# A two-layer encoder on 8 cores: transposes moved to the host, weight slabs stored contiguously, one projection reordered

## The chip, the cores and the metric

One Trainium2 chip, all 8 cores, each with its own 2048 tokens. The metric is device time in microseconds of the slowest core. In some executions the cores of one die, or of both, are granted a lower TensorE clock and the run is some per cent longer.

## The reference, cut to what matters

```python
D_MODEL, BATCH, SEQ, N_MEM, D_FF = 1024, 2, 8192, 256, 2816
# layer 0: conv mixer; layer 1: chunked spatial gating. Each layer:
x = x + mixer(rms_norm(x, g_mix))                       # in-proj, mixing, output projection
x = x + memory_cross_attention(rms_norm(x, g_xattn), rms_norm(mem, g_mem), w_q, w_k, w_v, w_o)
x = x + swiglu(rms_norm(x, g_ffn), w_gate, w_up, w_down)
# after both layers
out = rms_norm(x, g_final)                              # (2, 8192, 1024) float32
```

A core does its 2048 tokens in two halves of 1024, each half in two tiles of 512, with features on the partitions. x of a half stays in SBUF as `hT` (fp32), its norm as `nT` (bf16), and all weights are streamed once per half.

## The kernel before: the parts that matter

x comes in token by token, so every 128x128 block is transposed on TensorE and copied out of PSUM; the output goes the same way back.

```python
# load_x, tile(tb), one of 8 blocks of 128 tokens, each half hf of the features
ins = e.transpose(ps[:, i * 128:(i + 1) * 128], x.t[:, dc * 128:(dc + 1) * 128], self.ident[:, :])
...                                   # x.t: one of three staging buffers
P.add("act" or "dve", ...)            # copy PSUM -> hT   (shortened)
# store_pieces, piece(tt, tb): the same from nf, through PSUM and four staging buffers, to out
```

A weight slab is a block of columns cut out of a row-major matrix, cast to bf16 on its way, into one of a ring of four buffers. A load waits until the slab four places earlier has been used for the last time.

```python
NS = 4
def ld(self, w2d, c0, cw, kc, after=()):
    i = self.ws_i % NS
    ...
    src = w2d[:, c0:c0 + cw].rearrange("(k p) c -> p k c", p=128)
    self.P.add("pool", lambda e: e.dma_start(out=view, in_=src), ..., dma=f"w{i}")
```

The output projection of a mixer adds to `hT` and starts the next norm at once: squares on ScalarE and their sums on TensorE as each output block is done; after a tile's eighth block, "finish": Ln and Exp on ScalarE, eight scalings on VectorE.

```python
# proj_residual, inside block(slab, ss, s_, cw, tt), for each output block m of tile tt
self.residual_add(b, m, tt)                          # VectorE: hT += PSUM
self.push(j.key, lambda j=j, m=m: j.sq(m), lag)
if m == KC - 1 and not final:
    self.push_finish(j, lag)
...
block(sl0[0], sl0[1], 0, 512, 0)      # tile 0 with both slabs, then tile 1 with both
block(sl1[0], sl1[1], 1, 512, 0)
block(sl0[0], sl0[1], 0, 512, 1)
block(sl1[0], sl1[1], 1, 512, 1)
```

After this projection come the keys (8 groups), the values (4 groups) and the queries (16 groups) of the cross-attention. Keys and values need only the memory; the queries need the new norm. In the ring order the slabs are: two of the output projection, two of keys, two of values, two of queries.

The softmax here doesn't subtract the row's maximum and nothing guards it: scores larger than these inputs give would overflow.

Of the kernel before, what the change touches and what calls it, by code (L numbers as in the profile page):

```python
# [20 lines left out]
XROWS = TH + 2 * HALO  # L21
# [12 lines left out]

class Slot:
# [6 lines left out]

class Op:
    __slots__ = ("eng", "fn", "deps", "idx", "need_inc", "dma", "dma_val")

# [9 lines left out]

class Prog:
    ENGS = ("pe", "act", "dve", "pool", "sp")

    def __init__(self):
        self.streams = {e: [] for e in self.ENGS}  # L60
        self.dma_cnt = {}
        self.final_dma = set()

# [31 lines left out]
    EPOCH = 500  # L95

# [11 lines left out]
    def emit(self, nc, block, esem, dsem):  # L108
        def make(name):
            ops = self.streams[name]  # L110

            def body(e):
                waited = {}
                for o in ops:
# [8 lines left out]
                    for key, (val, h) in need.items():  # L123
                        if key[0] == "e":
                            later = [k for k in waited if k[0] == "e" and k[1] == key[1] and k[2] > key[2]]
                            if later:
                                continue
                        if waited.get(key, 0) < val:
                            e.wait_ge(h, val)
                            waited[key] = val  # L130
# [15 lines left out]

class Buf:
    __slots__ = ("t", "slot", "dma")

    def __init__(self, t, slot, dma=None):  # L150
        self.t = t
        self.slot = slot
        self.dma = dma

class Builder:
    def __init__(self):
# [10 lines left out]
        self.xb = {}  # L167
# [3 lines left out]
    def sb(self, name, shape, dtype):  # L171
        sz = 4 if dtype == F32 else 2
        n = 1
# [4 lines left out]
        self.off = off + n * sz  # L178
# [3 lines left out]
    def _declare_dram(self):  # L182
# [4 lines left out]
        self.x_in = din("x_in", [NHALF, XROWS, D])  # L187
        self.mem = din("mem", [NMEM, D])
        self.vecs = din("vecs", [128, NV])
        self.lnc = din("lnc", [3, D])  # L190
        self.od_w_s = din("od_w_s", [8, 128, 128])
        self.ev_w_in = din("ev_w_in", [D, 2560])
        self.ev_w_out = din("ev_w_out", [D, D])
        self.od_w_in = din("od_w_in", [D, 2048])
        self.od_w_out = din("od_w_out", [D, D])
        self.xa_w = {n: din("xa_w_" + n, [2, D, D]) for n in "qkvo"}
        self.ffn_w_gate = din("ffn_w_gate", [2, D, DFF])
        self.ffn_w_up = din("ffn_w_up", [2, D, DFF])
        self.ffn_w_down = din("ffn_w_down", [2, DFF, D])
        self.out = nc.dram_tensor("out", [TCORE, D], F32, kind="ExternalOutput").ap()  # L200

    def _alloc(self):
# [6 lines left out]
        self.hTh = self.sb("hTh", [128, KC, 2 * HALO], F32)  # L209
        self.hTh_s = [S(f"hTh{k}") for k in range(KC)]  # L210
        self.nTh = self.sb("nTh", [128, KC, 2 * HALO], BF16)
# [8 lines left out]
        self.diagA_s = S("diagA")  # L220
# [6 lines left out]
        self.xs = Ring([Buf(self.sb(f"xs{i}", [128, D], F32), S(f"xs{i}"), f"xs{i}") for i in range(3)])  # L227
# [4 lines left out]
        self.memnT_s = S("memnT")  # L232
        self.junk_s = S("junk")
# [11 lines left out]
        self.mst = self.sb("mst", [128, 2, D], F32)  # L245
        self.mst_s = [S(f"mst{i}") for i in range(2)]
        self.wst = self.sb("wst", [128, 2, 512], F32)
        self.wst_s = [S(f"wst{i}") for i in range(2)]
        self.junk = self.sb("junk", [128, D], BF16)
# [10 lines left out]
        self.xh = self.sb("xh", [2 * HALO, D], F32)  # L260
        self.xh_s = S("xh")
# [25 lines left out]
        self.os = Ring([Buf(self.sb(f"os{i}", [128, D], F32), S(f"os{i}"), f"os{i}") for i in range(4)])  # L287
        u_end = max(u_end, self.off)
        self.off = u_end
        self.union_slot = S("union")  # L290
# [39 lines left out]
    def norm_job(self, key, src_k, src_s, n, gcol, dst_k, dst_s):  # L330
# [3 lines left out]
        def sq(k):  # L334
            if st["b"] is None:
# [3 lines left out]
            ps = self.ps[b]  # L339
# [3 lines left out]
            P.add("act", lambda e: e.activation(out=q.t[:, 0:n], in_=src_k(k), func=AF.Square),  # L343
                  reads=[src_s[k]], writes=[q.slot])
            P.add("pe", lambda e: e.matmul(ps[:, 0:n], lhsT=self.ones[:, :], rhs=q.t[:, 0:n], start=first, stop=last),  # L345
                  reads=[q.slot, self.ones_s], writes=[self.ps_s[b]])
# [6 lines left out]
        def scale(k):  # L353
            r = st["r"]
            P.add("dve", lambda e: e.scalar_tensor_tensor(out=dst_k(k), in0=src_k(k),  # L355
                                                          scalar=self.vec[:, gcol + k:gcol + k + 1],
                                                          in1=r.t[:, 0:n], op0=ALU.mult, op1=ALU.mult),
                  reads=[src_s[k], r.slot, self.vec_s], writes=[dst_s[k]])
# [12 lines left out]
    def main_job(self, tt, gcol, final=False):  # L371
        sl = slice(tt * TT, (tt + 1) * TT)
        if final:
            return self.norm_job(("n", tt), lambda k: self.hT[:, k, sl], [self.hT_s[k][tt] for k in range(KC)], TT,
                                 gcol, lambda k: self.nf[tt][:, k, :], self.nf_s[tt])
        return self.norm_job(("n", tt), lambda k: self.hT[:, k, sl], [self.hT_s[k][tt] for k in range(KC)], TT,
                             gcol, lambda k: self.nT[:, k, sl], [self.nT_s[k][tt] for k in range(KC)])

    def union_switch(self, new_slots):
        pass  # L380
# [14 lines left out]
    def ld(self, w2d, c0, cw, kc, after=()):  # L395
# [3 lines left out]
        view = self.wbuf[i][:, 0:kc * cw].rearrange("p (k c) -> p k c", c=cw)  # L399
        src = w2d[:, c0:c0 + cw].rearrange("(k p) c -> p k c", p=128)  # L400
        self.P.add("pool", lambda e: e.dma_start(out=view, in_=src), reads=list(after), writes=[self.wbuf_s[i]],  # L401
                   dma=f"w{i}")
        return view, self.wbuf_s[i]

    def rstd_bc(self, b, n, scale, eps, extra_sub=None):
        ps = self.ps[b]
        t = self.t32.next()
        if extra_sub is not None:
            self.P.add("dve", lambda e: e.tensor_scalar(out=t.t[:, 0:n], in0=ps[:, 0:n], scalar1=scale, scalar2=eps,
                                                        op0=ALU.mult, op1=ALU.add),  # L410
                       reads=[self.ps_s[b]], writes=[t.slot])
            self.P.add("dve", lambda e: e.tensor_tensor(out=t.t[:, 0:n], in0=t.t[:, 0:n], in1=extra_sub.t[:, 0:n],
                                                        op=ALU.subtract),
                       reads=[t.slot, extra_sub.slot], writes=[t.slot])
            self.P.add("act", lambda e: e.activation(out=t.t[:, 0:n], in_=t.t[:, 0:n], func=AF.Ln),
                       reads=[t.slot], writes=[t.slot])
        else:
            ec = 0 if eps == RMS_EPS else 1
            self.P.add("act", lambda e: e.activation(out=t.t[:, 0:n], in_=ps[:, 0:n], func=AF.Ln, scale=scale,  # L419
                                                     bias=self.epsc[:, ec:ec + 1]),  # L420
                       reads=[self.ps_s[b], self.epsc_s], writes=[t.slot])
        r = self.rsr.next()
        self.P.add("act", lambda e: e.activation(out=r.t[:, 0:n], in_=t.t[:, 0:n], func=AF.Exp, scale=-0.5),  # L423
# [642 lines left out]
    def build(self):  # L1066
# [44 lines left out]
        for f in st:  # L1111
            f()
# [79 lines left out]
```

## Time and profile before

| | before |
|---|---|
| median of 4 runs (range) | 2027.06 us (2024.69 to 2047.15) |
| profiled run, slowest core (core 4) | 2022.6 us |
| TensorE busy on it | 93% |
| packets moved by DMA | 211481 |

The prediction shows the main lines. Three more of the timeline of core 4: two from the second tile's half of the layer-0 output projection, and one of the key matmuls behind it. Columns: start, length, engine, line, operation, operands, count, and in brackets the idle time just before and who ended it.

```profile
229.05 5.34 PE L389 MATMUL ps<-y,wbuf 128*128 128x512 bf16 x24 [2.21 <-ACT t L419]
237.18 0.38 PE L345 MATMUL ps<-sq,ones 128*128 128x512 bf16 x1 [0.42 <-ACT sq L343]
243.73 5.40 PE L389 MATMUL ps<-memnT,wbuf 128*128 128x256 bf16 x48
```

TensorE waits 2.21 us for a PSUM bank that ScalarE still has to read (the Ln of tile 0's norm). The queries start 22 us behind this projection.

### The profile page before, as it was taken

The numbers are of one execution on the slowest core, as the hardware profiler recorded it, in microseconds if no ns is written. First come the engines' busy times: TensorE is split into PE (matmuls) and PEld (weight loads), VectorE is DVE, ScalarE is ACT, GpSimd is POOL, SyncE is SP. The second block draws the span as 40 slices with busy tenths as digits, with TensorE's granted clock in tenths as the row PEclk, the third lists the DMA queues.
The fourth block names the chain that finished last, engine by engine and source line by source line (L and its number), as shares of the span: only waits on it lengthen the run. The fifth ranks groups of instructions, "written<-read, shape, count | busy, mean of one in ns | idle before, by whom it ended". The sixth has DMA issues, their size and how long they took to land.

```text
span 2022.6 us, 25188 instructions; the slowest of 8 cores (2007.9 to 2022.6 us)
## 1 busy us (share of the span) xinstructions
PE 1881.0 (93%) x8942; PEld 882.8 (44%) x9114; DVE 634.8 (31%) x988; ACT 598.9 (30%) x1001; POOL 178.2 (9%) x187
## 2 busy tenths in 40 slices
PE   5699999999989899999979999999998999999997
PEld 3344444444434444444444444444443444344444
DVE  2523415211156334211152432341212651531213
ACT  3323343111133352111152423521111433421112
POOL 6200000001100100001000001000010001000110
PEclk7899999999999999999989998999999999999998
DMA  8052582447736833549546048245497449245482
GB/s 203 7 78 37 76 118 42 65 66 73 81 61 84 114 54 55 71 63 87 68 140 84 1 63 125 42 58 71 60 89 90 61 64 134 32 63 84 50 86 83
DMA packets 211481, 150.91 MB, mean 75 GB/s; under 512 B 93024, under 2 KB 206816, under 8 KB 211360
## 3 DMA queue, kind: packets, MB, share of 16 engines
q0 software_dynamic: 205024, 130.03, 49.9%
q1 hardware_dynamic: 6336, 19.26, 2.8%
q8 instruction: 76, 1.25, 0.3%
q14 instruction: 45, 0.37, 0.1%
HBM read 270.92 MB, written 8.39 MB: 138 GB/s over the span
## 4 chain that ended last, share of the span: by engine, by line
PE 83%; ACT 5%; DVE 4%; DMA 4%; issue 3%; ACTq 0%; DVEq 0%; SPq 0%; POOLq 0%
PE ps L389 79%; DMA wbuf<-xa_w_q 3%; PE ps L345 2%; DVE nT L355 2%; DMA xs<-x_in 1%; ACT pT L983 1%; ACT L419 1%; ACT sq L343 1%; PE ps L607 1%; ACT t L419 1%; DVE nf L355 1%; PE ps L706 1%; ACT t L995 0%; ACT rs L423 0%; DMA out<-os 0%
## 5 line engine op out<-in xcount | busy, mean ns | idle before, releaser
L389 PE MATMUL ps<-nT,wbuf 128*128 128x512 bf16 x4135 | 933.5, 383 | 26.7 <-DMA wbuf<-xa_w_q 12.4
L389 PEld LDWEIGHTS ps<-nT,wbuf 128*128 128x128 bf16 x4224 | 414.3, 99 | 519.6 <-issue 40.6
L389 PE MATMUL ps<-hid,wbuf 128*128 128x512 bf16 x1376 | 311.3, 379 | 1.5
L343 ACT ACTIVATE sq<-hT 128x512 bf16<-128x512 f32 x224 | 137.0, 626 | 451.5 <-DVE hT L444 439.8
L1035 DVE TENSOR_TENSOR hid<-ps,t 128x512 bf16<-128x512 f32 x176 | 121.0, 691 | 469.2 <-PE ps L389 469.2
L444 DVE TENSOR_TENSOR hT<-hT,ps 128x512 f32<-128x512 f32 x192 | 130.8, 687 | 383.9 <-PE ps L389 365.3
L1033 ACT ACTIVATE t<-ps 128x512 f32<-128x512 f32 x176 | 104.7, 597 | 474.4 <-PE ps L389 474.3
L389 PEld LDWEIGHTS ps<-hid,wbuf 128*128 128x128 bf16 x1408 | 137.8, 98 | 165.7
L355 DVE SCALAR_TENSOR_TENSOR nT<-hT,vec,rs 128x512 bf16<-128x512 f32 x192 | 133.6, 763 | 52.4 <-ACT rs L423 52.4
L389 PE MATMUL ps<-y,wbuf 128*128 128x512 bf16 x504 | 122.6, 391 | 9.4 <-ACT t L419 8.8
L389 PE MATMUL ps<-oT,wbuf 128*128 128x512 bf16 x504 | 117.9, 379 | 9.2 <-DVE oT L1005 4.8
L345 PE MATMUL ps<-sq,ones 128*128 128x512 bf16 (+1 forms) x232 | 82.7, 374 | 34.2 <-ACT sq L343 31.8
L389 PE MATMUL ps<-a_ext,diagA 128*128 128x512 bf16 x484 | 107.0, 379 | 0.8 <-issue 0.2
L1005 DVE TENSOR_TENSOR oT<-ps,rs 128x512 bf16<-128x512 f32 x64 | 41.1, 686 | 199.3 <-PE ps L389 127.3
L389 PEld LDWEIGHTS ps<-y,wbuf 128*128 128x128 bf16 x512 | 51.1, 100 | 73.8 <-issue 17.3
L389 PEld LDWEIGHTS ps<-oT,wbuf 128*128 128x128 bf16 x512 | 49.5, 98 | 70.1 <-issue 12.2
L401 POOL DMA_DIRECT2D wbuf<-ffn_w_gate x24 | 21.0, 876 | 648.1 <-PE ps L389 648.1
L389 PEld LDWEIGHTS ps<-a_ext,diagA 128*128 128x128 bf16 x496 | 48.0, 97 | 58.7
L401 POOL DMA_DIRECT2D wbuf<-ffn_w_down x32 | 43.0, 1344 | 281.3 <-PE ps L389 142.0
L389 PE MATMUL ps<-wbuf,nT 128*128 128x512 bf16 x252 | 60.0, 399 | 7.6 <-DVE nT L355 7.3
L966 ACT ACTIVATE qT<-ps 128x512 bf16<-128x512 f32 x64 | 38.2, 597 | 92.2 <-PE ps L389 92.2
L345 PEld LDWEIGHTS ps<-sq,ones 128*128 128x128 bf16 x240 | 23.7, 99 | 70.4 <-issue 48.3
(114 smaller groups left out, 1053.1 us busy)
## 6 DMA issues: line engine op xcount, KB each, us to landing
wbuf<-ffn_w_down POOLq DMA_DIRECT2D x32, 704.0 KB, 9.8
wbuf<-ffn_w_gate POOLq DMA_DIRECT2D x20, 1024.0 KB, 11.2
wbuf<-ffn_w_up POOLq DMA_DIRECT2D x20, 1024.0 KB, 14.8
xs<-x_in SPq DMA_DIRECT2D x16, 512.0 KB, 6.1
wbuf<-xa_w_k POOLq DMA_DIRECT2D x8, 1024.0 KB, 11.2
wbuf<-xa_w_v POOLq DMA_DIRECT2D x8, 1024.0 KB, 10.2
wbuf<-xa_w_q POOLq DMA_DIRECT2D x8, 1024.0 KB, 14.8
wbuf<-xa_w_o POOLq DMA_DIRECT2D x8, 1024.0 KB, 20.3
```

The source lines that it names most:

```text
L343: P.add("act", lambda e: e.activation(out=q.t[:, 0:n], in_=src_k(k), func=AF.Square), reads=[src_s[k]], writes=[q.slot])
L345: P.add("pe", lambda e: e.matmul(ps[:, 0:n], lhsT=self.ones[:, :], rhs=q.t[:, 0:n], start=first, stop=last), reads=[q.slot, self.ones_s], ...
L355: P.add("dve", lambda e: e.scalar_tensor_tensor(out=dst_k(k), in0=src_k(k), scalar=self.vec[:, gcol + k:gcol + k + 1], in1=r.t[:, 0:n], op ...
L389: ins = e.matmul(ps[:, 0:n], lhsT=l, rhs=r, start=(i == 0), stop=(i == np_ - 1))
L401: self.P.add("pool", lambda e: e.dma_start(out=view, in_=src), reads=list(after), writes=[self.wbuf_s[i]], dma=f"w{i}")
L419: self.P.add("act", lambda e: e.activation(out=t.t[:, 0:n], in_=ps[:, 0:n], func=AF.Ln, scale=scale, bias=self.epsc[:, ec:ec + 1]), reads= ...
L444: self.P.add("dve", lambda e: e.tensor_tensor(out=self.hT[:, m, sl], in0=self.hT[:, m, sl], in1=ps[:, :], op=ALU.add), reads=[self.ps_s[b] ...
L607: ins = e.transpose(ps[:, i * 128:(i + 1) * 128], x.t[:, dc * 128:(dc + 1) * 128], self.ident[:, :])
L966: P.add("act", lambda e, b=b, m=m, sl=sl: e.activation(out=self.qT[:, m, sl], in_=self.ps[b][:, :], func=AF.Copy), reads=[self.ps_s[b]], w ...
L1005: P.add("dve", lambda e, b=b, oc=oc: e.tensor_tensor(out=self.oT[:, 2 * hh + oc, sl], in0=self.ps[b][:, :], in1=rs.t[:, :], op=ALU.mult), ...
L1033: P.add("act", lambda e, t=t, bg=bg: e.activation(out=t.t[:, :], in_=self.ps[bg][:, :], func=AF.Silu), reads=[self.ps_s[bg]], writes=[t.slot])
L1035: P.add("dve", lambda e, t=t, bu=bu, f=f, sl=sl: e.tensor_tensor(out=self.hid[:, f, sl], in0=self.ps[bu][:, :], in1=t.t[:, :], op=ALU.mult ...
```

## The change

Its intent: take all transposes off TensorE by handing over x, the memory and the chunk weights already transposed (and taking the output transposed); shorten the weight loads by storing each slab as one contiguous run per partition; and use slab 0 of a mixer's output projection on both tiles before slab 1. The instructions were also moved into shorter helpers, which changes no work but changes the line numbers: TensorE's L389 is L401 in the changed kernel, and many engines' operations carry L72, the line of a helper.

```diff
-            src = w2d[:, c0:c0 + cw].rearrange("(k p) c -> p k c", p=128)
+        flat = self.wbuf[i][:, 0:kc * cw]
+        src = w[layer, off:off + kc * 128 * cw].rearrange("(p f) -> p f", p=128)
 ...                                             # in proj_residual
-            block(sl0[0], sl0[1], 0, 512, 0)
-            block(sl1[0], sl1[1], 1, 512, 0)
-            block(sl0[0], sl0[1], 0, 512, 1)
-            block(sl1[0], sl1[1], 1, 512, 1)
+            order = [(i, tt) for tt in range(NTT) for i in range(2)]
+            if name in ("ev_out", "od_out"):
+                order = [(i, tt) for i in range(2) for tt in range(NTT)]
 ...                                             # load_x, its transposes and buffers go
+    def load_tile(self, h, tt):
+        for k in range(0, KC, 2):
+            self.P.dma("sp", f"x{tt}_{k}", (), [self.hT_s[k][tt], self.hT_s[k + 1][tt]],
+                       out=self.hT[:, k:k + 2, tt * TT:(tt + 1) * TT], in_=self.x_in[h, tt, :, k:k + 2, :])
 ...                                             # in l0_mixer: first weights wait for x's third pair
+        g = () if self.diag_done else [self.hT_s[5][0]]
 ...                                             # store_pieces goes; nf is stored as it is
+                self.P.dma("sp", nm, [self.nf_s[tt][k - 1], self.nf_s[tt][k]], (),
+                           out=self.out[h, tt, :, k - 1:k + 1, :], in_=self.nf[tt][:, k - 1:k + 1, :])
```

## The prediction

> **What bounds the kernel now.** I read four views in this order: the page's busy line, the stage table (busy time by stretch, with the TensorE clock), the list of what TensorE waited for, and the timeline at the places that list names. All are of core 4, the slowest.
>
> ```profile
> PE 1881.0 (93%) x8942; PEld 882.8 (44%) x9114; DVE 634.8 (31%) x988; ACT 598.9 (30%) x1001; POOL 178.2 (9%) x187
> PE   5699999999989899999979999999998999999997
> ```
> TensorE (PE) is the bound nearly everywhere; it thins out in slices 1 and 2, about slice 21, in small dips, and in the last slice. In the chain that ended last, a steady stretch looks like this (start, length, what):
>
> ```profile
> 345.19 10.74 PE ps L389 x49
> 355.98 10.74 PE ps L389 x49
> ```
> 49 matmuls of 128x512 per 10.79 us, some 0.22 us each at full clock. (Longer groups, such as 121 convolution matmuls in 26.8 us with three records missing, give 0.2155.) The change cannot touch those. The stage table (length; busy of PE, weight load, DVE, ACT, POOL; clock; DMA):
>
> ```profile
> 0.00:98.40 98.40, 57.22 (x311) 32.30 (x317) 36.91 (x64) 36.85 (x67) 43.45 (x51) 0.81 0.45 104
> 247.00:1001.00 754.00, 727.70 (x3370) 332.82 (x3436) 220.56 (x333) 205.49 (x342) 60.13 (x61) 0.99 0.59 74
> 1001.00:1083.50 82.50, 62.31 (x371) 37.61 (x376) 38.00 (x67) 40.70 (x73) 1.89 (x3) 0.88 0.31 94
> 1998.00:2022.60 24.60, 11.75 (x68) 10.39 (x66) 14.14 (x21) 11.50 (x18) 0.00 (x0) 0.74 0.43 171
> ```
> Four stretches: the start up to the first convolution matmul; the body; the turn between the two halves; the tail. The start and the turn hold the large holes and a clock of 0.81 and 0.88. What TensorE waited for (total, times, longest):
>
> ```profile
> PE ps L345 <- ACT sq L343: 31.8, 17, 7.1
> PE ps L607 <- DMA xs<-x_in: 15.4, 4, 6.3
> PE ps L389 <- DVE nT L355: 15.2, 3, 7.9
> PE ps L389 <- ACT t L419: 12.6, 8, 2.2
> PE ps L389 <- DMA wbuf<-xa_w_q: 12.4, 4, 3.4
> PE ps L571 <- DVE mst L561: 6.9, 2, 3.7
> PE ps L706 <- DVE nf L355: 5.5, 3, 2.0
> ```
> L607, L706 and L571 are transposes of input, output and memory on TensorE; L345 sums squares for the norms. Only input x and the query weights xa_w_q cost real DMA waits.
>
> **What the skill says.** (1) "TensorE: Matmul & The Clock Gate", Part 1: a PE idle for some 3.4 us falls to half clock and needs about as long busy to come back. The trace agrees: at 35.66, after 7.87 us idle, 7 matmuls took 3.19 us, twice 0.2155 each. (2) The same page, Part 4: a transpose by identity costs about 275 to 390 ns. Here, in a stream at full clock, 24 took 2.78 us, so about 0.107 each; the trace decides. (3) "DMA: Bandwidth & Descriptors", Why small descriptors are slow: each carries a fixed overhead. Weight pieces here land as 1 KB packets; at the xa_w_q wait the engines were saturated (share 1.14) at 161 GB/s of bf16, 322 of fp32 read. (4) "SBUF — State Buffer", Who interferes with whom: a VectorE operation with two SBUF inputs and a GpSimd operation reading SBUF shut each other out. The trace agrees: four norm scalings took 4.95 us at 51.40, while POOL built diagonals, against 2.73 at 32.41 with POOL idle.
>
> **The change, part by part.** The host now hands over x, memory and w_s already transposed, and each weight slab contiguous; x is loaded straight into hT, nf is stored straight to out. Instruction counts: PE 9114 to 8826, exactly the 288 transposes (128 of x, 128 of nf, 16 memory, 8 w_s, 16 halo, less 8 new square sums for memory). All other matmuls remain. ACT goes from 956 to 918 and DVE from 988 to 968, mostly PSUM copies; both have slack. My floor is 8162 N=512 matmuls x 0.2155 = 1759 us plus some 44 for small ones; the 280 full transposes x 0.107 = 30 us come on top and go. They are counted inside the stages below, not again.
>
> *Start, now 98.4.* Before: x trickles through three buffers, nT of tile 0 is ready and the first projection starts at 35.66. After: four 512 KB loads fill tile 0, queued first, with the weight loads held until its third pair lands. In the turn the store queue reached 356 to 388 GB/s and in the start 252; 2.1 MB from about 2.5 us lands at about 9.5. Then last squares 1.1, their matmuls 0.9, Ln and Exp 1.3, eight scalings of 0.68 = 5.4, some slowed by POOL: nT at about 19.5. Held weights share the DMA with tile 1, memory and the bias, so the gate slab lands at 20 to 23. First projection at 20. From there before took 62.7 us for some 36 of work; after, work is 128 x 0.2155 + 8 squares 1.7 + halo and memory about 3 = 32.5. The 7.1 us halo wait (a PSUM copy queued behind DVE), the 6.9 us of memory waits and about 2 of w_s go. I keep 2 for the gate slab, 4 for tile 1's nT slowed by POOL, 5 for cold clock: 44. First convolution at 64, gain 34.
>
> *Turn, now 1005.5 to 1083.5.* Before: the first projection at 1035.06, then 48.4 us. After: nf of tile 0 ends at 1014.2 as now and its last pair of x is issued then, lands about 1019; squares, Ln, Exp to 1022.4, eight scalings: nT and first projection at 1028.3. Then 31.6 of work (the 32.5 without memory's squares), 2 cold, 3 waits: about 1065. That is 6.7 gained up to the first projection, because no store or input transpose stands before it in TensorE's queue, and 11.8 after it, from the 32 input transposes (3.4), the 3.45 us wait for x, the 3.18 us halo wait and the clock. Tile 1 of x queues behind 2.1 MB of stores, so of 18.5 I count 17.
>
> *Tail, now 24.6.* nf ends at 2012.2 either way; now transposes and copies run to 2018.4. After, the last store goes out at about 2012.3 but 4 MB leave in 10 us; at the 405 GB/s seen at 2016 they just about keep up. End about 2017.5: gain 5.
>
> *Query weights.* Issue of the first xa_w_q slab is tied to the end of the first xa_w_k slab by the four-buffer ring, before and after:
>
> ```profile
> 241.77 0.88 POOL L401 DMA_DIRECT2D wbuf<-xa_w_v  x1 [7.69 <-PE ps L345]
> 246.18 0.88 POOL L401 DMA_DIRECT2D wbuf<-xa_w_q  x1 [3.54 <-PE ps L389]
> 259.15 29.20 PE L389 MATMUL ps<-nT,wbuf 128*128 128x512 bf16 x125 [3.11 <-DMA wbuf<-xa_w_q]
> wbuf<-xa_w_q POOLq DMA_DIRECT2D x8, 1024.0 KB, 14.8
> ```
> Two slabs, 4.2 MB of fp32, take from about 243.7 to 258.9, 276 GB/s. With 16 KB runs I estimate 320 to 350 (from 44 ns per 256-byte packet of ffn_w_down, 7.8 us x 16 / 2816, and about 115 per 1 KB one: 20 fixed + 0.093 per byte, so 17% of a 1 KB packet is overhead). Then they need 12 to 13 us, and the wait of 3.1 drops below 0.5. Each wait also cooled the clock: 125 matmuls took 29.20 instead of 26.94, on average 2.5 per case. Four cases x (3.1 + 2.5) = 22; I count 18, and 1.5 for xa_w_v.
>
> *Output projection of both mixers.* Its order becomes slab-major. Now tile 1's first group meets the bank of tile 0's norm while ACT loads a table and takes Ln: 2.21, four times. In the new order the group that meets that bank comes one group (1.7 us) later, so about 0.7 is left: gain 6. Both norms then finish later, but some 15 us of key and value matmuls lie before the queries.
>
> Sum: 34 + 17 + 5 + 18 + 1.5 + 6 = 81.5. From 2027.06: 1945.6.
>
> **Rivals.** *A: DMA is the start's bound.* In the start the engines run at shares of about 1 from 5 to 40 us; if x only spreads the same 8 MB and the weights, held back, arrive at 28 instead of 20, the start gains 24. For it: the share. Against: the first 2.1 MB are alone in the queue. Time 1956. *B: the query waits stay.* If fp32 reads at HBM, not packets, set 276 GB/s, the 18 shrinks to 3: about 1961. For it: single slabs land in 9.4 to 10.2 already. Against: 256-byte packets are plainly slower per byte. *C: transposes were hidden.* If the freed TensorE time only lengthens waits for DVE norms (15.2 us now), the turn gains 8 and the start 20: 1969. *D: all comes out, with no stall for tile 1:* 1932.
>
> **Range and chances.** The start is uncertain by 8, the turn 6, queries 6, projection 3, tail 3: combined about 12, and 1.3 of these each way makes 1929 to 1966. 2% is 1986.5, which needs half the gain to fail: faster 0.95, same 0.045, slower 0.005.
>
> **What would show it.** First projection near 20 and first convolution near 64; in the turn, projection near 1028 less what was gained; no PE wait for xa_w_q over 1 us; weight slabs landing about 2 us sooner; steady groups unchanged at 49 per 10.79 us. It is wrong if x loads land late, if weight DMAs with long runs are slower, or if new waits on norm banks appear.

## The result, and the profile after

| | before | after |
|---|---|---|
| median us (range, runs, slow ones included) | 2030.63 (2024.69 to 2300.85, 16) | 1965.06 (1961.49 to 2316.51, 11); its seven fast ones alone 1962.9 |
| ratio, with 95% interval | | 0.9674 (0.963 to 0.9717) |
| profiled run, slowest core | 2022.6 | 1961.5 |

A ratio is the mean time of one kernel's fast runs over that of the other's fast runs of the same rounds, so it isn't quite the ratio of the medians quoted. The kernel is faster by 3.3%. 1965 lies in the predicted range of 1929 to 1966, but at its very edge: 19 us of the expected gain of 81.5 did not come. That it lies inside is luck: the prediction's own working, 1.3 times 12 each way of 1945.6, ends at 1961; the range is 5 us wider there.

The page of core 2, the slowest:

```profile
PE 1832.0 (93%) x8654; PEld 840.0 (43%) x8826; DVE 622.6 (32%) x968; ACT 573.9 (29%) x959; POOL 118.3 (6%) x194
DMA packets 28949, 150.60 MB, mean 77 GB/s; under 512 B 2976, under 2 KB 3360, under 8 KB 17440
```

The weight loads (PEld) fell by 288 and VectorE's instructions by 20, as counted, ScalarE's by 42 (38 counted; two of the other four are table loads, 43 to 41), and 211481 packets became 28949 for the same bytes. What was to go is gone.

The stages tell where the time went. Each row is the mean over the eight cores of the profiled run, from one landmark on TensorE to the next (the first convolution matmul, the first matmul of an output projection, the first query matmul, the first sum of exponentials, and, as "last square", the last square of tile 0 at the end of a half). Rows with "x4" are sums over two layers and two halves.

| stage | before | after | gained | predicted |
|---|---|---|---|---|
| start to first convolution | 99.4 | 66.5 | 32.9 | 34 |
| output projection, keys, values x4 | 209.1 | 204.9 | 4.2 | } 25.5 |
| queries x4 | 123.4 | 119.2 | 4.2 | } (18 + 1.5 + 6) |
| turn: last square to convolution | 78.3 | 61.6 | 16.7 | 17 |
| tail: last square to the end | 25.0 | 18.0 | 7.0 | 5 |
| convolution or gating to output projection x4 | 341.9 | 344.7 | -2.8 | 0 |
| whole span | 2017.5 | 1954.8 | 62.7 | 81.5 |

The rows sum to 62.2; all other stages agree within 0.5. All waits for query slabs lie in the second row; what the third row lost before, and gained, is cold clock behind them, that is TensorE at work with half its clock granted (4.2 us before, 0 after; counted below). So 17 of the missing 19 us are in one place, between the first matmul of the mixers' output projections and the end of the queries. The stage table of core 2 for the start, the turn and the tail (columns as in the prediction):

```profile
0.00:70.60 70.60, 41.90 (x221) 17.96 (x226) 26.51 (x36) 28.12 (x55) 43.38 (x52) 0.88 0.51 119
973.20:1040.80 67.60, 43.35 (x237) 18.69 (x241) 29.94 (x54) 29.80 (x53) 1.52 (x3) 0.80 0.44 134
1944.00:1961.50 17.50, 1.00 (x3) 0.10 (x1) 11.38 (x17) 4.43 (x6) 0.00 (x0) 0.57 0.62 240
```

TensorE's busy time fell from 57.22 to 41.90 in the start and from 62.31 to 43.35 in the turn, while the stretches shrank by 28 and 15 us (core 4 before, core 2 after): both were filled with the transposes and with the waits around them. What TensorE waited for on core 2:

```profile
PE ps L72 <- ACT sq L72: 52.0, 23, 11.0
PE ps L401 <- DVE nT L72: 16.3, 4, 7.2
PE ps L401 <- DMA wbuf<-w_ev_in: 12.7, 2, 10.0
PE ps L401 <- ACT t L72: 5.6, 8, 0.9
PE ps L401 <- DMA wbuf<-w_xq: 0.8, 2, 0.4
```

Read this against the list of before. The waits for queries fell from 12.4 to 0.8 and those for the Ln's bank from 12.6 to 5.6, as predicted. But the waits for squares rose from 31.8 to 52.0. These two lists are of different cores: on the mean of the eight it is 31.5 to 46.4, and 14.0 of these 14.9 us are in the four output projections (0.8 to 14.8; the rest of core 2's rise is mostly in its turn). Nobody had counted them. The timeline shows where they come from. TensorE of core 2 in the layer-0 output projection and after it:

```profile
210.99 1.89 PE L401 MATMUL ps<-y,wbuf 128*128 128x512 bf16 x8 [0.48 <-ACT t L72]
215.87 0.38 PE L72 MATMUL ps<-sq,ones 128*128 128x512 bf16 x1 [0.82 <-ACT sq L72]
219.12 0.43 PE L72 MATMUL ps<-sq,ones 128*128 128x512 bf16 x1 [2.87 <-ACT sq L72]
219.34 7.06 PE L401 MATMUL ps<-memnT,wbuf 128*128 128x256 bf16 x48
233.70 27.79 PE L401 MATMUL ps<-nT,wbuf 128*128 128x512 bf16 x125 [0.40 <-DMA wbuf<-w_xq]
```

The other engines in the same stretch:

```profile
211.67 2.74 DVE L72 SCALAR_TENSOR_TENSOR nT<-hT,vec,rs 128x512 bf16<-128x512 f32 x4 [2.31 <-ACT rs L72]
213.42 0.53 POOL L75 DMA_DIRECT2D wbuf<-w_xv  x1 [15.43 <-PE ps L401]
214.92 2.74 DVE L72 SCALAR_TENSOR_TENSOR nT<-hT,vec,rs 128x512 bf16<-128x512 f32 x4
217.57 0.69 DVE L72 TENSOR_TENSOR hT<-hT,ps 128x512 f32<-128x512 f32 x1
218.34 0.63 ACT L72 ACTIVATE sq<-hT 128x512 bf16<-128x512 f32 x1 [2.61 <-DVE hT L72]
223.45 0.53 POOL L75 DMA_DIRECT2D wbuf<-w_xq  x1 [9.50 <-PE ps L401]
```

Tile 0 is now done just before tile 1's last blocks. VectorE takes its work in program order: eight scalings for tile 0's norm (2.74 us for each four), and only behind them, at 217.57, the last residual add of tile 1. Its square and the sum on TensorE come after that. ScalarE itself sat idle for 2.61 us before that square, until VectorE's add, so it isn't what was late. That makes 0.48, 0.82 and 2.87 us of waiting, 4.2 us in place of the 2.6 of before. And TensorE is slow behind the stall: the 48 key matmuls at 219.34 took 7.06 us, against 5.40 before. And there is a second reading in these lines. The first query slab was issued 10.0 us behind the second value slab (223.45 against 213.42); before it was 4.4 (246.18 against 241.77, in the prediction). TensorE's stall holds up the key matmuls, whose end frees the query slab's buffer, but not the value load. So the value slab has the queue nearly to itself, and then so has the query slab. The query wait may be gone because of the stall, not because of the layout. That is the question that the runs had to settle.

### The profile page after: what moved, and what is told of

Its sections match the earlier page's. It is cut to its first block, busy times and chain, and to the rows that moved or that the text cites. A ratio compares the mean times of both kernels' runs of the same rounds, so it can differ in the third digit from the quotient of the medians.

```text
span 1961.5 us, 24385 instructions; the slowest of 8 cores (1950.7 to 1961.5 us)
## 1 busy us (share of the span) xinstructions
PE 1832.0 (93%) x8654; PEld 840.0 (43%) x8826; DVE 622.6 (32%) x968; ACT 573.9 (29%) x959; POOL 118.3 (6%) x194
## 2 busy tenths in 40 slices
DMA packets 28949, 150.60 MB, mean 77 GB/s; under 512 B 2976, under 2 KB 3360, under 8 KB 17440
## 4 chain that ended last, share of the span: by engine, by line
PE 85%; DVE 5%; ACT 4%; issue 3%; DMA 3%; DVEq 0%; ACTq 0%; SPq 0%; POOL 0%; POOLq 0%
PE ps L401 82%; DVE nT L72 3%; PE ps L72 2%; ACT t L72 1%; DMA wbuf<-w_xq 1%; DMA wbuf<-w_ev_in 1%; ACT L72 1%; DMA hT<-x_in 1%; ACT pT L72 1%; DVE nf L72 1%; ACT sq L72 1%; DVE hT L72 0%; ACT rs L72 0%; DVE t L72 0%; PE ps L733 0%
## 5 line engine op out<-in xcount | busy, mean ns | idle before, releaser
L401 PE MATMUL ps<-nT,wbuf 128*128 128x512 bf16 x4132 | 925.8, 381 | 27.5 <-DMA wbuf<-w_ev_in 12.7
L401 PEld LDWEIGHTS ps<-nT,wbuf 128*128 128x128 bf16 x4224 | 412.1, 98 | 517.0 <-issue 33.9
L72 ACT ACTIVATE t<-ps 128x512 f32<-128x512 f32 (+1 forms) x288 | 164.0, 574 | 564.8 <-PE ps L401 536.8
L401 PE MATMUL ps<-hid,wbuf 128*128 128x512 bf16 x1376 | 311.3, 379 | 1.5
L72 ACT ACTIVATE sq<-hT 128x512 bf16<-128x512 f32 x224 | 137.4, 627 | 468.9 <-DVE hT L72 443.0
L72 DVE TENSOR_TENSOR hid<-ps,t 128x512 bf16<-128x512 f32 x176 | 121.0, 691 | 468.8 <-PE ps L401 468.8
L72 DVE TENSOR_TENSOR hT<-hT,ps 128x512 f32<-128x512 f32 x192 | 131.3, 687 | 388.9 <-PE ps L401 366.4
L401 PEld LDWEIGHTS ps<-hid,wbuf 128*128 128x128 bf16 x1408 | 137.8, 98 | 165.7
L72 DVE SCALAR_TENSOR_TENSOR nT<-hT,vec,rs 128x512 bf16<-128x512 f32 x192 | 135.9, 776 | 73.0 <-ACT rs L72 73.0
L72 PE MATMUL ps<-sq,ones 128*128 128x512 bf16 (+2 forms) x242 | 86.2, 379 | 52.6 <-ACT sq L72 52.0
L401 PE MATMUL ps<-oT,wbuf 128*128 128x512 bf16 x504 | 117.9, 379 | 9.2 <-DVE oT L72 4.8
L401 PE MATMUL ps<-y,wbuf 128*128 128x512 bf16 x502 | 118.8, 379 | 2.6 <-ACT t L72 1.9
L401 PE MATMUL ps<-a_ext,diagA 128*128 128x512 bf16 x484 | 107.0, 378 | 0.7
L72 DVE TENSOR_TENSOR oT<-ps,rs 128x512 bf16<-128x512 f32 x64 | 41.1, 686 | 182.7 <-PE ps L401 155.1
L401 PEld LDWEIGHTS ps<-oT,wbuf 128*128 128x128 bf16 x512 | 49.5, 98 | 70.1 <-issue 12.2
L401 PEld LDWEIGHTS ps<-y,wbuf 128*128 128x128 bf16 x512 | 49.8, 98 | 63.3 <-issue 3.8
L72 ACT ACT_TABLE_LOAD x41 | 52.6, 1283 | 74.8 <-PE ps L72 22.8
L401 PEld LDWEIGHTS ps<-a_ext,diagA 128*128 128x128 bf16 x496 | 48.0, 97 | 58.7
L401 PE MATMUL ps<-wbuf,nT 128*128 128x512 bf16 x252 | 60.9, 403 | 7.6 <-DVE nT L72 7.3
L72 PEld LDWEIGHTS ps<-sq,ones 128*128 128x128 bf16 x248 | 24.5, 100 | 91.6 <-issue 69.5
L72 ACT ACTIVATE qT<-ps 128x512 bf16<-128x512 f32 x64 | 38.2, 597 | 73.7 <-PE ps L401 73.7
L75 POOL DMA_DIRECT2D wbuf<-w_fg x24 | 12.7, 528 | 637.7 <-PE ps L401 637.7
## 6 DMA issues: line engine op xcount, KB each, us to landing
wbuf<-w_xq POOLq DMA_DIRECT2D x8, 1024.0 KB, 11.7
```

Source lines behind the costliest of these rows:

```text
L72: return self.add(eng, lambda e: getattr(e, meth)(**kw), reads, writes)
L75: return self.add(eng, lambda e: e.dma_start(**kw), reads, writes, dma=sem)
L401: ins = e.matmul(ps[:, 0:n], lhsT=l, rhs=r, start=(i == 0), stop=(i == np_ - 1))
```

## The experiments

Theory: the new order stalls the projection on VectorE, and this stall, spacing the loads out, is what ended the query waits. Rival: the contiguous layout ended them, as predicted, and the stall is a separate loss. All edits are against the changed kernel unless they say so; in each, the output was right, but for one kernel that says otherwise. Medians include slow runs unless the row says so. They ran in three groups; the kernel before took 2028.12, 2027.91 and 2029.44 us (medians) beside them.

| run | what it is | median us | ratio to before (95%) | span, mean of cores |
|---|---|---|---|---|
| the changed kernel | | 1965.06 | 0.9674 (0.963 to 0.9717) | 1954.8 |
| tile_major | old order | 1970.41 | 0.9723 (0.9701 to 0.9745) | 1956.2 |
| strided_weights | old layout | 1970.39 and 1973.4, the two fast runs of 5 | none given | 1963.9 |
| late_finish | both norms finished at the end | 1951.09 | 0.9625 (0.9605 to 0.9644) | 1939.6 |
| hold_rest | tile 1 behind the first weights | 1969.32 | 0.9715 (0.9693 to 0.9737) | 1964.5 |
| five_only | fifth weight buffer | 1962.06, 1958.04, 1959.33, the fast runs of 6 | 0.9659 (0.9639 to 0.9678) | 1955.7 |
| tile_five | old order, fifth buffer | 1951.88 | 0.9623 (0.9607 to 0.9639) | 1948.6 |
| late_five | late_finish, fifth buffer | 1938.91 | 0.9562 (0.9547 to 0.9576) | 1933.7 |
| no_turn_stores | no stores in the turn | 1961.6, one run | none | 1956.2 |
| late_five_strided | late_five, old layout | 1944.12 | 0.9581 (0.9545 to 0.9617) | 1938.9 |
| late_five_nogate | late_five, first weights not held | 1939.62 | 0.956 (0.9532 to 0.9588) | 1933.0 |

The next table was worked out from the kept traces: means over the eight cores, summed over the four places (two layers, two halves), from the first matmul of the output projection to the end of the queries. "Gap" is the time from the issue of the second value slab to that of the first query slab, "landing" from the issue of the query slab until it has landed, "ready" from its issue until TensorE could start the queries; these three are means of one place. "Cold clock" is TensorE's busy time times the share of its clock that was not granted (nearly always half).

| run | gap | landing | ready | query wait | Ln's bank wait | squares' wait | cold clock | length |
|---|---|---|---|---|---|---|---|---|
| before | 4.4 | 13.0 | 10.5 | 11.1 | 8.8 | 0.8 | 7.8 | 332.5 |
| changed kernel | 9.6 | 9.2 | 9.9 | 0.4 | 1.9 | 14.8 | 5.7 | 324.1 |
| tile_major | 4.4 | 11.3 | 9.9 | 6.2 | 8.8 | 0.9 | 7.5 | 325.2 |
| strided_weights | 9.6 | 10.2 | 10.1 | 2.2 | 1.9 | 14.8 | 6.8 | 327.4 |
| late_finish | 4.4 | 11.7 | 9.9 | 7.7 | 0 | 0.3 | 3.3 | 312.8 |
| tile_five | 8.2 | 9.5 | 14.1 | 0 | 8.8 | 0.8 | 4.5 | 314.8 |
| late_five | 15.5 | 9.5 | 14.4 | 0 | 0 | 0.3 | 2.0 | 302.2 |

**tile_major: the old order, with all else of the change.**

```diff
-            if name in ("ev_out", "od_out"):
-                order = [(i, tt) for i in range(2) for tt in range(NTT)]
```

> The changed kernel with one thing undone: the output projections of both mixers go tile by tile again, as before the change. Theory 1 (the slab-by-slab order costs time, because the last residual additions of tile 1 queue on VectorE behind the eight scalings of tile 0's norm, and TensorE waits 0.82 and 2.87 us for the last two squares, four times): those two waits go, the old wait of about 2.2 us for Ln comes back, so some 1.5 to 2 us are won per place and the time falls by 6 to 9 us, from about 1962 to about 1954. Query weights wait under 1.5 us each. Theory 2 (the order is what lets the value slabs start early, and so ended the query waits): the waits for query weights come back at 2 to 3 us each and the time rises by 3 to 10 us.

The time rose as theory 2 said, the waits came back, but the reason that theory 2 gives (value slabs start early) falls with late_finish below. Here the layout stands alone, and it does not end the query waits; it about halves them. Per core they sum to 12.2, 5.0, 9.5, 3.8, 1.1, 9.2, 0.2 and 8.2 us, a mean of 6.2, against 11.1 before (6.4 to 12.9) and 0.4 in the changed kernel. The weight queue of core 0, and its first query matmul:

```profile
213.60 0.53 POOL L75 DMA_DIRECT2D wbuf<-w_xv  x1 [7.46 <-PE ps L72]
218.14 0.53 POOL L75 DMA_DIRECT2D wbuf<-w_xq  x1 [4.01 <-PE ps L401]
```

```profile
231.28 29.11 PE L401 MATMUL ps<-nT,wbuf 128*128 128x512 bf16 x128 [3.24 <-DMA wbuf<-w_xq]
```

From the issue of the value slab to the arrival of the query slab it is 17.7 us on this core with runs of 16 KB; on core 4 before, with runs of 2 KB, it was 17.4 (241.77 to 259.15). But core 0 is the worst: on the mean of cores and places the query slab had landed 15.7 us after the value slab's issue (14.0 to 17.3 by core), against 17.4 before (15.8 to 18.2). So the layout does speed the pair up, by 1.7 us, and still not enough: the query slab lands 11.3 us after its issue and TensorE is ready after 9.9. On core 4, whose wait was 1.1, it is 15.5:

```profile
226.31 27.79 PE L401 MATMUL ps<-nT,wbuf 128*128 128x512 bf16 x125 [1.09 <-DMA wbuf<-w_xq]
```

One core of each adjacent pair (0 and 1, 2 and 3, and so on) waits 8.2 us or more and the other 5.0 or less, so the spans split into 1944 to 1950 and 1965 to 1968, and the slowest core sets the time. The mean over cores is that of the changed kernel within 1.4, though the median is 5 us longer (7.5 against the changed kernel's fast runs alone). In a second run of it the long ones were cores 1, 2, 4 and 6 instead of 0, 2, 5 and 7. The Trainium skill ("HBM Reference", Specifications) says that two cores of a domain share its bandwidth; that adjacent numbers make a pair is my reading of the pattern, not shown. In all four pairs the core that issued its first query slab earlier, counted from its own start, waited less for its query slabs; in late_finish it was so in three of four. No run tested that as a cause.

**strided_weights: the old layout, with all else of the change.**

```diff
-        src = w[layer, off:off + kc * 128 * cw].rearrange("(p f) -> p f", p=128)
+        src = w[layer][:, c0:c0 + cw].rearrange("(k p) c -> p k c", p=128)
 ...          # destination viewed to match; the host passes the arrays as they are
```

> The changed kernel with the weights left in their original row-major layout and read in pieces of 128 to 512 columns; everything else as changed. If the contiguous layout is what ended the query waits: they come back at 2.5 to 3.5 us each with their cold clock, slabs land 2 us later, the first slabs of the start land some 2 to 4 us later, and the time rises by 15 to 28 us, to 1977 to 1990. If the layout does nothing (the rate is set by reading fp32 from memory): the time stays within 4 us and query waits stay under 1 us.

With the old 2 KB runs and the new order the query waits are nearly gone all the same: 0 to 5.5 us per core, a mean of 2.2. The waits of core 0, its worst:

```profile
PE ps L401 <- DMA wbuf<-w_ev_in: 16.0, 1, 16.0
PE ps L401 <- DMA wbuf<-w_xq: 5.5, 3, 2.3
```

So this run fits neither of its two expectations: the waits are nearly gone, yet the two fast runs are 5 to 8 us longer than the changed kernel's median. The order took away more of the query waits than the layout did (11.1 to 2.2, against 11.1 to 6.2), and both together left 0.4. With the stall's gap of 9.6 us the query slab lands 10.2 us after its issue even in the old layout, just when TensorE is ready (10.1). What the layout really buys is in the first line: without it the first projection starts at 30.2 us instead of 23.2 and the first convolution at 73.2 instead of 66.5. The stages are from a fast run.

**late_finish: the new order, but neither norm is finished before both tiles are done.**

```diff
                 if m == KC - 1 and not final:
-                    self.push_finish(j, lag)
+                    if name not in ("ev_out", "od_out"):
+                        self.push_finish(j, lag)
+                    elif tt == NTT - 1:
+                        for jj in jobs:
+                            self.push_finish(jj, lag)
```

> The changed kernel with the slab-by-slab order kept, but the finish of tile 0's norm (Ln, Exp, eight scalings) recorded after the last square of tile 1. Theory 1 (VectorE's order is the cause): the waits for squares of 0.82 and 2.87 us fall under 0.5 each; a wait of up to 2 us for Ln on a bank may come in their place; the time falls by 6 to 12 us. Rival (the squares are late because ScalarE is busy with Ln, Exp and its table load, or because of the residual additions themselves): the waits stay over 2 us in sum per place and the time stays within 3 us.

This takes the stall away, and the query waits come back: a mean of 7.7 us per core (1.9 to 11.5), with the contiguous layout in place. Core 0:

```profile
210.12 0.53 POOL L75 DMA_DIRECT2D wbuf<-w_xv  x1 [15.01 <-PE ps L72]
212.08 0.38 PE L72 MATMUL ps<-sq,ones 128*128 128x512 bf16 x1 [0.33 <-ACT sq L72]
214.79 0.53 POOL L75 DMA_DIRECT2D wbuf<-w_xq  x1 [4.14 <-PE ps L401]
227.93 8.25 PE L401 MATMUL ps<-nT,wbuf 128*128 128x512 bf16 x24 [3.29 <-DMA wbuf<-w_xq]
```

The 2.87 before the last squares is 0.33, and the query slab follows the value slab by 4.7 us again, as before (4.4), and costs 3.29, as before (3.11). The first value slab is issued as early as in the changed kernel (15.5 us before the second, there 16.0), and TensorE is ready equally long after the issue (9.9 us on the mean), but the query slab takes 11.7 us to land and not 9.2. So the theory holds: in the changed kernel one wait had taken the place of the other. (The edit moves ScalarE's Ln and Exp too; that VectorE and not ScalarE made the squares late is read from the idle time above.) The median fell by 14 us, more than the 6 to 12 expected. Projection, keys and values fell from 204.9 to 190.4 us, the queries rose from 119.2 to 122.4.

**five_only, late_five and tile_five: a fifth weight buffer, alone, with late_finish, and with the old order.** The fifth buffer frees the query slab from the key slab: it then waits for the end of the output projection.

```diff
-NS = 4
+NS = 5
```

> The changed kernel with only a fifth weight buffer. Theory (in the changed kernel the query slabs are on time because TensorE stands still for the squares meanwhile, so there is no weight wait left to take away): time within 4 us of the changed kernel, 1959 to 1966, waits for squares still 3.7 us per place. Rival (late slabs still cost something in the changed kernel, in the projection of the start or elsewhere): 5 us or more faster.

> The changed kernel with the late finish of tile 0's norm and a fifth weight buffer. Without the waits for squares, the query slabs were waited for again on most cores (up to 11.5 us in sum). Theory (the ring of four ties the first query slab to the end of the first key slab and puts it behind the second value slab in the queue; a fifth buffer lets it be issued at the end of the output projection): no wait for query weights over 0.5 us on any core, the stretch from output projection to scores falls from 313 us to 305 to 307 on the mean of the cores, spans agree within some 8 us, and the time is 1934 to 1940. Rival (two cores share a memory and the later of the two is starved whatever the buffers do): waits over 1.5 us stay on some cores and the time stays within 4 us of 1951.

> The changed kernel with the old tile-by-tile order of the output projections and a fifth weight buffer. Theory (in the old order the only thing lost to the late kernel is the wait for query weights on the slower core of each pair, plus 2.2 us for Ln four times): query waits under 0.5 us on all cores, the time falls from 1970 to 1945 to 1950. Rival (the rate of the DMA, not its place in the ring, sets the query wait): waits of 2 to 3 us stay on the slower cores and the time stays at 1963 to 1971.

Alone the buffer changes nothing (projection to values 205.1, queries 119.6, mean span 1955.7 against 1954.8): the changed kernel's loss is the stall, not the ring. By the table it is 14.5 us of waits for squares, 1.9 for the bank and 3.7 of cold clock. With late_finish it takes the query waits away on all eight cores. Core 0 of late_five:

```profile
207.56 0.53 POOL L75 DMA_DIRECT2D wbuf<-w_xq  x1 [15.01 <-PE ps L72]
221.92 14.41 PE L401 MATMUL ps<-nT,wbuf 128*128 128x512 bf16 x66
```

The slab is asked for 14.4 us ahead of its first matmul instead of 9.9 (late_finish: 214.79 to the 224.64 at which TensorE was ready), and nothing is in brackets behind the matmul. The buffer also puts the query slab 15.5 us behind the value slab; no run separates the early issue from this spacing. Projection to values fell to 182.0, queries stand at 120.2: together 302.2 against 324.1 (expected 305 to 307), which is the gain of 22 that the change had left lying. At 1938.91 us it beats both kernels, and the changed one by some 1.2% (0.9562 over 0.9674). In tile_five (1951.88, where 1945 to 1950 was expected) the waits for queries are gone too and the two-way split of the cores with them (spans 1946.5 to 1950.2), but the norm's waits of the old order stay: 12.6 us for the Ln's bank on core 0, as before, and 195.6 from projection to values. The old order with the late finish was not run, so it stays open whether the new order is needed at all.

**late_five_strided: the old layout on top of late_five.** The edit is that of strided_weights.

> The fastest version so far (late finish, fifth buffer), with the weights left in their original layout. It measures what the contiguous layout is worth once neither a stall nor the ring hides it. Theory (the layout matters at the start, where the first slabs share the DMA engines with x, and hardly in the body): the first projection starts near 31 us instead of 23, the query waits stay under 0.5 us per place, the time rises by 6 to 10 us, from 1939 to 1945 to 1949. Rival of the prediction (the layout is what ends the query waits): they come back at 1.5 us or more per place and the time rises by 15 us or more.

Still no query wait on any core, and projection to the end of the queries takes 300.3 against 302.2. The intervals of the two ratios overlap, so the loss is read from the stages: the mean span is 5.2 us longer, and the start 7.4 (first projection at 29.9 against 22.8 us). With an early enough load the layout does nothing for the queries.

**hold_rest: is the start set by the order of its loads?** Tile 1 of x, the halo, the memory and the bias wait for the first two weight slabs.

```diff
-        for tt in range(NTT):
-            self.load_tile(0, tt)
-        self.load_halo(0)
-        self.setup_dma()
+        self.load_tile(0, 0)
 ...                                  # in l0_mixer, behind the first two weight loads
+            self.load_tile(0, 1, after=[sva[1], sga[1]])
+            self.load_halo(0)
+            self.setup_dma()
```

> The changed kernel with the loads of tile 1, the halo, the memory and the bias held until the first two weight slabs have landed. Theory (in the start the two first slabs share the DMA engines with 3.7 MB that is not needed yet): the first slabs land near 18 and 21 us, the first projection starts at 22.6 with nT instead of 24.9, the 2.7 us wait for the second slab goes, the first convolution matmul comes at 64 to 67 instead of 70.6, and the time falls by 4 to 7 us. Rival (the DMA is the bound of the whole start, so the order only moves the wait): tile 1's squares are waited for instead, and the first convolution stays within 2 us of 70.6.

My expectation of a gain fell. Core 4:

```profile
22.52 3.57 PE L401 MATMUL ps<-nT,wbuf 128*128 128x512 bf16 x8 [7.85 <-DVE nT L72]
35.95 1.10 PE L72 MATMUL ps<-sq,ones 128*128 128x512 bf16 x2 [9.86 <-ACT sq L72]
```

The wait for the weight slab is gone from the first projection, but it starts only at 22.1 (23.2 in the changed kernel), and then TensorE waits 9.9 us for tile 1, and the convolution starts at 74.4 instead of 66.5. **late_five_nogate** asks the same from the other side: the first weights are no longer held for x.

```diff
-        g = () if self.diag_done else [self.hT_s[5][0]]
+        g = ()
```

> The fastest version so far, with the first two weight slabs no longer held until the third pair of x has landed. Theory 1 (the whole start is bound by the DMA engines, so what goes first only moves the wait): the first projection comes 1 to 4 us later because tile 0 of x lands later, the wait for the second slab goes, and the first convolution stays within 2 us of 66. Theory 2 (the held slabs are what the start waits for): the first convolution comes 3 us or more earlier and the time falls below 1937.

First projection 22.3 (22.8 in late_five; theory 1 had it 1 to 4 us later, which fell), convolution 67.2 against 66.0, the waits for `w_ev_in` down from 5.2 to 0.2 us, the time the same. Putting tile 1 last costs 8 us, and dropping the hold on the weights about nothing. That fits a start that depends on all the bytes that it has to bring in; the order in the changed kernel is already about as good as these. In the changed kernel the DMA engines of core 2 are busy for a share of 0.93 from 2.5 to 10 us, 1.01 to 25 and 0.91 to 40, and 0.01 from there to the convolution: the transfers fill the first 40 us, and what follows is mostly TensorE's own work (busy for 26.0 of 30.6 us).

**no_turn_stores: are the stores in the way of x in the turn?** This kernel leaves out the stores of the first half, so its output is wrong (half of it is never written, and the error is not a number).

```diff
-            if k % 2 == 1:
+            if k % 2 == 1 and load is None:
```

> The changed kernel without the stores of the first half's output (wrong on purpose: half of the output is never written). Theory (in the turn x lands late because the stores of tile 0 share the DMA engines): the first projection comes 22.5 to 23 us after the last square of the previous half instead of 24.9, and the turn takes 58 to 60 instead of 61.6. Rival (x is late because its four loads are issued one by one as VectorE frees hT, and their own latency is all): the turn stays within 1 us of 61.6.

Nothing moved: the turn took 62.3 us (61.6 with the stores) and its first projection came 25.0 us after the last square (24.9). But the test isn't clean: without the stores the loads of tile 1 are issued from 10.1 us after the last square on, instead of from 12.0 to 14.2, and take their place on the engines while tile 0's last pair is landing. All that is shown is that dropping the stores alone gains nothing. What delays the first projection stands in the changed kernel's timeline of core 2, the load queue and ScalarE:

```profile
982.51 4.54 SPq L75 DMA_DIRECT2D hT<-x_in  x4
```

```profile
988.01 1.15 ACT L72 ACTIVATE sq<-hT 128x512 bf16<-128x512 f32 x2 [4.12 <-DMA hT<-x_in]
993.02 3.36 ACT L72 ACTIVATE sq<-hT 128x512 bf16<-128x512 f32 x6 [3.86 <-DMA hT<-x_in]
```

Four loads take 4.54 us to issue one behind the other; the first pair's squares start 5.5 us after its issue, and those of the second only at 993.02, 10.5 us after the first issue. Before, the first three blocks had been fetched ahead into the staging buffers that the change removed. On the mean of the cores the fourth pair was issued 8.8 us after the last square, as reckoned (8.7), but had landed at 15.6, not 13.5; without the stores at 15.7. A weight slab issued at 0.7 us, until about 6 us, and tile 1's loads share the engines with these pairs; what each costs, no run tells.

## Why the prediction was right or wrong

**Right: the start, 32.9 gained for 34.** But 6.7 of the 32.9 are the layout's (66.5 against 73.2 in strided_weights), which the prediction named as a gain for the queries only. First projection at 23.2 for 20: x's fourth pair landed at 11.9 to 13.9 us, not at 9.5, and on five of the eight cores the norm was what ended the wait. On the other three it was the first weight slab, on core 2 until 24.91; the gate slab, the second one, landed at 25.8 to 31.6 for 20 to 23 and cost core 2 another 2.7 (rival A in small). The stretch behind the first projection took 43.3 for 44.

```profile
24.91 3.48 PE L401 MATMUL ps<-nT,wbuf 128*128 128x512 bf16 x8 [10.02 <-DMA wbuf<-w_ev_in]
```

**Right: the turn, 16.7 for 17.** Up to the first projection 4.6 of the 6.7, as x landed 2 us late; behind it 12.2 for 11.8. **The tail, 7.0 for 5**: the stores did keep up with VectorE (on core 2 the span ends 3.5 us after the last scaling, 1958.0). **Right: the steady groups** did not change. Rival C (the transposes were hidden) is out by its numbers (20 and 8 us for start and turn); no run put the transposes back, so that they and their waits were on the path there is read from the stages. The weight slabs landed some 2 us sooner, as said (medians 14.8 to 11.7 us for queries, 11.2 to 9.8 for gates; core 4 before, core 2 after).

**Wrong: the "Query weights" and "Output projection" terms, 18 + 1.5 + 6 = 25.5 expected, 8.4 measured.** Two steps failed, and a third was mis-sized. Of the waits that were to go, 18.9 us did go (query slabs 10.6, value slabs 1.4, Ln's bank 6.9), but 14.0 us of waits for squares came, and of the cold clock only 2.1 went.

1. "With 16 KB runs I estimate 320 to 350 ... Then they need 12 to 13 us, and the wait of 3.1 drops below 0.5." Measured alone (tile_major) and on the mean of the cores, the layout brought the two slabs from 15.4 to 13.7 us in the prediction's count, which starts 2 us behind the issue; that is some 307 GB/s. Half the query waits stayed (6.2 of 11.1), and the stretch of projection and queries gained 7.3 of the 19.5 (332.5 to 325.2). The waits in the changed kernel did drop below 0.5, so its own test ("no PE wait for xa_w_q over 1 us") passed, for another reason than the one given. Rival B was nearer, though its 3 us for the layout are too few.

2. "In the new order the group that meets that bank comes one group (1.7 us) later, so about 0.7 is left: gain 6." The bank wait did fall, 2.21 to 0.48 on core 2, 6.9 in sum. But "Both norms then finish later, but some 15 us of key and value matmuls lie before the queries" looked only at who needs `nT`. It missed that the eight scalings now stand ahead of tile 1's last residual adds in VectorE's queue, and that TensorE's own sum of squares waits for these. 2.2 + 0.4 of waiting became 0.5 + 0.8 + 2.9, and the clock cold behind it. (New waits at the norms were among the prediction's own signs of being wrong.) The order alone, by itself a loss from projection to values (202.5 to 204.9 with the contiguous layout), spaced the two loads out from 4.4 to 10 us, and this ended the query waits.

3. The cold clock behind each query wait, counted as 2.5 a case or 10 in all, was 4.2 in all before (mean of the cores). The prediction set 29.20 us for 125 query matmuls against 26.94; but there are 128, with three records missing, and without a wait they take 27.8 (27.79 behind 0.40 or 1.09 in the lines above, 29.11 behind 3.24). So waits and cold clock of the query slabs cost 11.1 + 4.2 = 15.3 us together, less than the 18 that were to be gained from them.

The two failures lie on each other: alone the layout gained 7.3 here, the order (strided_weights) 5.1 (332.5 to 327.4), both 8.4, because both act on the same query waits. That all of it could be had is shown by late_five: 302.2 against 332.5 is 30.3, with the two causes taken away one by one.

**Not foreseen: -2.8 from the convolution or gating to the output projection.** The waits there are the same before and after within 0.2 us. The difference is cold clock: 3.0 us lost before, 5.8 after (4.1 to 7.1 in the other variants of the table, whose lengths of 342.9 to 345.9 follow it). In the convolution stretch the loss comes in pieces of 1.7 us, 3.4 us at half clock each, in 3 of 16 cases before and 9 of 16 after. Why they became more frequent no run tells.

## What to carry to other kernels

When a wait goes away, look at what the loads in front of it did before you credit the change that was meant for it: a stall that delays one issue can hide a slow transfer, and removing one alone gains only a part (here 11 of the 22 us for the stall, in late_finish, and nothing for the ring, in five_only). When you reorder matmuls, walk through the queues of the engines that follow them: work that is "needed later" still stands in front of work that is needed now. And start a load early rather than make it faster: one more buffer in the ring with the norms kept out of the way gained 22 us here, while 7 times fewer packets were worth 5 to 9 (mean spans of late_five and of the changed kernel, with and without the layout), mostly in the start.

## What the Trainium skill lacked or had wrong

- "TensorE: Matmul & The Clock Gate", Part 4: it gives about 275 to 390 ns for a 128x128 transpose in bf16, as the time of one. One fp32 transpose lasts 329 to 341 ns on the mean in the trace of before, which agrees; what the page lacks is the rate of a stream of transposes: at full clock 24 took 2.78 us, about 0.11 us each. Taken as a rate its figure would have made the 30 us of transposes 77 to 109.
- "DMA: Bandwidth & Descriptors", Why small descriptors are slow: not wrong here. Its count of 3 cycles on top of one per 32 bytes makes an estimate of 9% for the 1 KB packets of a query slab, where the prediction had taken 17% from landing times. With the load order unchanged (tile_major) the two slabs landed in 15.7 us on the mean for 17.4 before, 10% less; the page was nearer.
- "DMA: Bandwidth & Descriptors", Anatomy of one DMA: its fit of 2.0 us plus bytes over 436e3 gives an estimate of 6.8 us for the 2.1 MB of fp32 behind one slab; on core 2 of the changed kernel the medians were 8.3 (values), 9.8 (gates) and 11.7 (queries), with a cast to bf16, other loads in the queue and all cores running.
- "HBM Reference", Specifications: it says that each core gets about its share when both of a pair stream. If adjacent numbers are a pair, which is not shown, tile_major doesn't look like even shares: one core of each waited 8.2 to 12.2 us for its query slabs and the other 0.2 to 5.0, with spans of 1944 to 1950 against 1965 to 1968 us, and which one changed from run to run. No run measured the bandwidth of each core.
- No page says that a stall can hide a slow load by spacing the loads out: 3.7 us of waiting for squares at each place opened the gap between two slabs from 4.4 to 10 us, and the query wait fell from 11.1 to 2.2 us per core in the old layout, to 0.4 in the new one.
